# The last feed-forward's output product as seven block products of half size, with raw activations

## The chip, the cores and the metric

The kernel runs on one core of one Trainium2 chip. Its engines are named as in the profile: PE is the matrix engine (TensorE) and PEld its weight load, DVE the vector engine, ACT the scalar engine, POOL the GpSimd engine, SP the sync engine. SP and POOL issue the DMAs here. The metric is the time of one execution on the device in microseconds; three runs of the kernel before the change had a median of 1910.15 us (1910.07 to 1911.91).

## What is computed

A decoder trunk of two layers on 512 tokens of width 1024. Each layer is a half-step SwiGLU feed-forward, a mixing sub-layer (attention, RWKV-7, short convolution), and a second half-step feed-forward. Before each stands an RMS norm with a scale and shift from the conditioning vector c (adaLN); a gate from c scales what is added to the residual h.

```python
for l in range(DEPTH):                    # 2
    mod = (silu(c) @ w_ada[l] + b_ada[l]).reshape(B, 9, D_MODEL)
    ...
    hn = rms_norm(h, g_ffn2[l]) * (1.0 + sc3) + sh3
    h = h + 0.5 * (1.0 + gt3) * swiglu(hn, w_ffn2_in[l], w_ffn2_out[l])

def swiglu(x, w_in, w_out):               # 1024 -> 2 x 2816 -> 1024
    gate, up = split(x @ w_in, 2)
    return (silu(gate) * up) @ w_out
```

All data are float32.

## The kernel before

Everything is kept transposed: features on the 128 partitions, the 512 tokens along the free axis. h is eight tiles of 128 x 512; the 2816 inner features are 22 row tiles (NF), taken two at a time as 11 pairs.

A float32 product is made of three passes in the faster type fp32r. Weights and activations are each split into a high part (a cast on ACT, L104, or L455 and L557 for activations) and the rest (a subtraction on DVE, L105, or L456 and L558). The three matmuls are high x high, high weight x low activation, and low weight x high activation (`mm3`, L93 to L95; `mm6`, L101; `prod`, L449 to L451). So each weight tile costs a DMA into `wraw`, an ACT cast into `wH` and a DVE subtraction into `wL`; `wH` and `wL` have four buffers each, `wraw` has two.

A feed-forward (`ffn`, L370) works in two groups (GROUPS: row tiles 0 to 11, then 12 to 21). In each group it first makes the activations. The first two pairs (four in the very first feed-forward) go through plain products of 512 tokens (L538 to L559). Every later pair goes through `pair_in` (L458), which already forms its input product from seven block products instead of eight (a scheme of the Strassen kind): halves of the input features against halves of the tokens, 24 matmuls of 256 columns for each. For it, sums of weight blocks are made on the way in: a plain DMA on SP (`raw`), then a DMA on the POOL queue that adds a second block to it (`plus`, L403). The seventh product of a pair (`rest`, L515) is delayed into the next pair by `waiting` and `flush`. The pair's activations are split at once by `put` (L454) and kept as `actH` and `actL`.

Then the group multiplies its activations by the output weights (L578 to L591): for each of the eight output tiles, 12 or 10 row tiles times three matmuls of 512 columns into one PSUM bank, then a DVE update of h (`residual`, L315) with the gate `cg`. In the second group the last two output tiles go through `close` (L326) in token halves of 256 columns. Output tile by output tile, the first group also computes some rows of the adaLN vectors for later sub-layers (`ada_steps`, L176): POOL issues a load of 128 x 1024 weights `wada` into one of three buffers, and DVE makes a dot product of it (L168). `need` says how many rows must be done before a sub-layer ends.

The code names engines and tiles; a scheduler that runs when the program is built sets the order of each engine's queue, from dependences, buffers and its own estimates. Each engine then executes its queue strictly in order and waits on semaphores.

Of the kernel before, what the change touches and what calls it, by code (L numbers as in the profile page):

```python
# [16 lines left out]
P = 128  # L17
# [43 lines left out]
def trunk_kernel(ctx, tc, ins, out, layers=L, phases=("ffn1", "mix", "ffn2")):  # L61
# [308 lines left out]
    def ffn(l, w_in, w_pair, w_out, hn, im, ss, need, then, ready, first=None, late=None):  # L370
# [6 lines left out]
        with tc.tile_pool(name="act", bufs=1) as ap_:  # L377
            com = {n: tuple(ap_.tile([P, 4, H2], F32R, name=x, tag="com", bufs=8) for x in ("comH", "comL")) for n in ("P1", "P2", "T3", "T4")}
            ap_.tile([P, (512 - GAP) // 4], F32, name="gap", tag="gap")
            n_first = 2 if first is None else 4  # L380
            tiles = (t for t in projector([w_in[l, j, g] for j in range(2 * n_first) for g in range(2)], hn, BANKS[:3], first, 1, ready) if t is not None)
            xs, waiting, done, after = {}, [], [None], [None]
# [19 lines left out]
            def plus(w, src):  # L402
                nc.gpsimd.dma_start(w, src, accum_op=ALU.add)  # L403

            def new_x(p):

                X = tuple(ap_.tile([P, 2, T], F32R, name=x, tag="act", bufs=12) for x in ("actH", "actL"))
# [4 lines left out]
            rows_, sums = [], {}  # L412

            def whole(n):

                for k in (2 * n, 2 * n + 4):
                    x = ap_.tile([P, 2, T], F32, name="x", tag="act", bufs=12)
# [35 lines left out]

            def put(X, sl, x):  # L454
                nc.scalar.copy(X[0][:, :, sl], x)  # L455
                return tt(X[1][:, :, sl], x, X[0][:, :, sl].bitcast(F32), ALU.subtract)  # L456

            def pair_in(p):  # L458
# [52 lines left out]
                act(s2, s2, AF.Silu)  # L511
                tt(up, s2, up, ALU.mult)
                put(X, hi_, up)

                def rest():  # L515
                    prod(pD, hl(raw(A(1, 1))), T4, False)
                    tt(gate, pD, gate, ALU.mult)
                    return put(X, lo_, gate)

                waiting.append(rest)  # L520

            turn_ = [0]
# [12 lines left out]
            crep = ada_crep(ap_) if n_first == 4 else None  # L535
            for g, (j0, j1) in enumerate(GROUPS):
                for p in range(j0 // 2, j1 // 2):
                    if p < n_first:  # L538
                        X = new_x(p)
                        for j in (2 * p, 2 * p + 1):  # L540
# [13 lines left out]
                            else:  # L554
                                act(s, pg, AF.Silu)
                                stt(s, s, -1.0, pu, ALU.mult, ALU.mult)
                                nc.scalar.copy(xs[j][0], s)  # L557
# [4 lines left out]
                    else:  # L562
                        after[0] = None if g or p > n_first + 1 else loads[-2]
                        pair_in(p)
                        after[0] = None
                flush()
                if g and ss is not None:
# [768 lines left out]
    for n, (l, p) in enumerate(seq):  # L1336
# [25 lines left out]
    for i in range(KD):  # L1362
        nc.sync.dma_start(out[i], h[i])


def lay_out(i):
# [18 lines left out]
    for n, w in (("w1o", "w_ffn1_out"), ("w2o", "w_ffn2_out")):  # L1385
        a[n] = c(i[w].reshape(L, NF, P, KD, P).transpose(0, 3, 2, 1, 4))


# [62 lines left out]
```

## Time and profile before

| what | us |
|---|---|
| median of three runs | 1910.15 |
| the profiled execution: its span, first to last instruction | 1906.7 |
| the last feed-forward's pairs of the first group begin | 1607.4 |
| its first output group | 1685.35 to 1750.64 |
| its second group's pairs | 1750.64 to 1847.47 |
| its second output group, 512 columns | 1847.47 to 1888.28 |
| the same in `close`, 256 columns | 1888.28 to 1902.56 |

Times in the profile count from the span's start. A row of the table by stretch gives, for each engine, its busy time and instructions in that stretch, then the granted PE clock, the mean busy share of the 16 DMA engines, and what they moved in GB/s. A row of a group gives an instruction's line, engine, operation, tiles and shapes, its count, and behind the bar its busy time and the mean of one in ns, then the idle time before and what ended it.

### The profile page before, as it was taken

What the parts mean: (1) busy time and instruction counts of PE and PEld (TensorE: products, weight loads), DVE (VectorE), ACT (ScalarE), POOL (GpSimd) and SP (SyncE); (2) the same over time, 40 slices, a digit from 0 to 9 for tenths busy, and PEclk for the clock granted to TensorE, in tenths of its full rate; (3) what the DMA queues carried; (4) which work ended last, traced back from release to release, by engine and by line L of the source; (5) the groups of instructions that cost most, each with busy time, mean ns of one, the idle gap of its engine ahead of it and who ended that gap; (6) DMA issues with size and microseconds to landing.
All of it is one profiled execution on the core that took longest, in us unless ns stands there. A gap on an engine that the chain in (4) does not pass through costs nothing. (4 is left out here: it accounts for less than half of the span.)

```text
span 1906.7 us, 37156 instructions
## 1 busy us (share of the span) xinstructions
PE 1880.9 (99%) x15540; PEld 1742.4 (91%) x15540; DVE 1406.9 (74%) x2192; ACT 844.7 (44%) x1272; POOL 130.8 (7%) x212
## 2 busy tenths in 40 slices
PE   9999999999999999999999999999999999999999
PEld 8998899897889999899899989989877999988998
DVE  6797687858876877677777776877598777864862
ACT  4453355346432554155345524544553335532551
POOL 0101100000000000110100021010000000110000
PEclk8999999999999999999999999999999999999999
DMA  7667877421222476886717678781221306774741
GB/s 301 231 187 234 258 197 238 160 70 45 74 64 65 119 203 173 281 220 191 274 59 188 172 260 246 192 271 53 89 63 43 108 24 170 203 221 130 194 140 60
DMA packets 105864, 308.48 MB, mean 162 GB/s; under 512 B 23392, under 2 KB 26464, under 8 KB 104672
## 3 DMA queue, kind: packets, MB, share of 16 engines
q1 hardware_dynamic: 77472, 203.33, 32.6%
q0 software_dynamic: 28224, 102.77, 21.7%
q8 instruction: 122, 2.00, 0.4%
q14 instruction: 46, 0.38, 0.1%
HBM read 302.66 MB, written 3.41 MB: 161 GB/s over the span
## 5 line engine op out<-in xcount | busy, mean ns | idle before, releaser
L104 ACT CAST wH<-wraw 128x1024 fp32r<-128x1024 f32 (+2 forms) x292 | 268.5, 922 | 472.8 <-PE ps_mm L94 165.9
L105 DVE TENSOR_TENSOR wL<-wraw,wH 128x1024 fp32r<-128x1024 f32 (+2 forms) x292 | 308.3, 1059 | 99.5 <-ACT wH L104 98.6
L93 PE MATMUL ps_mm<-actH,wH 128*128 128x512 f32 (+1 forms) x784 | 288.6, 368 | 0.0
L94 PE MATMUL ps_mm<-actL,wH 128*128 128x512 f32 (+1 forms) x784 | 288.1, 368 | 0.0
L95 PE MATMUL ps_mm<-actH,wL 128*128 128x512 f32 (+1 forms) x784 | 288.1, 367 | 0.0
L449 PE MATMUL ps_d<-comH,wH 128*128 128x256 f32 x816 | 227.0, 278 | 1.9 <-ACT wH L104 0.8
L451 PE MATMUL ps_d<-comH,wL 128*128 128x256 f32 x816 | 225.9, 277 | 2.3 <-DVE wL L105 2.3
L450 PE MATMUL ps_d<-comL,wH 128*128 128x256 f32 x816 | 225.6, 277 | 0.0
L168 DVE SCALAR_TENSOR_TENSOR wada<-wada,crep 128x1024 f32<-128x1024 f32 x140 | 167.7, 1220 | 47.0 <-DMA wada<-in_wadaT 46.7
L101 PE MATMUL ps_mm<-hnH,wL 128*128 128x256 f32 x976 | 199.8, 283 | 0.5 <-DVE wL L105 0.5
L101 PE MATMUL ps_mm<-hnH,wH 128*128 128x256 f32 x976 | 197.7, 283 | 0.5 <-ACT wH L104 0.3
L101 PE MATMUL ps_mm<-hnL,wH 128*128 128x256 f32 x976 | 197.2, 281 | 0.0
L105 DVE TENSOR_TENSOR wL<-sum,wH 128x1024 fp32r<-128x1024 f32 x102 | 124.9, 1224 | 72.7 <-ACT wH L104 72.5
L95 PEld LDWEIGHTS ps_mm<-actH,wL 128*128 128x128 f32 x784 | 147.8, 189 | 24.5
L94 PEld LDWEIGHTS ps_mm<-actL,wH 128*128 128x128 f32 x784 | 147.8, 189 | 24.2
L93 PEld LDWEIGHTS ps_mm<-actH,wH 128*128 128x128 f32 x784 | 147.8, 189 | 24.0
L104 ACT CAST wH<-sum 128x1024 fp32r<-128x1024 f32 x102 | 107.5, 1054 | 136.0 <-PE ps_d L450 53.4
L449 PEld LDWEIGHTS ps_d<-comH,wH 128*128 128x128 f32 x816 | 153.3, 188 | 4.3 <-ACT s L487 1.8
L101 PEld LDWEIGHTS ps_mm<-hnH,wL 128*128 128x128 f32 x976 | 149.8, 188 | 7.9 <-issue 6.7
L101 PEld LDWEIGHTS ps_mm<-hnH,wH 128*128 128x128 f32 x976 | 148.9, 188 | 8.3 <-issue 5.1
L451 PEld LDWEIGHTS ps_d<-comH,wL 128*128 128x128 f32 x816 | 153.2, 188 | 2.9 <-DVE wL L105 2.9
L101 PEld LDWEIGHTS ps_mm<-hnL,wH 128*128 128x128 f32 x976 | 149.6, 188 | 5.2 <-issue 4.9
(433 smaller groups left out, 4338.4 us busy)
## 6 DMA issues: line engine op xcount, KB each, us to landing
wada<-in_wadaT POOLq DMA_DIRECT2D x128, 512.0 KB, 5.0
wraw<-in_wmi SPq DMA_DIRECT2D x40, 512.0 KB
wraw<-in_w2p SPq DMA_DIRECT2D x36, 512.0 KB
wraw<-in_w1p SPq DMA_DIRECT2D x32, 512.0 KB
wraw<-in_w1o SPq DMA_DIRECT2D x32, 384.0 KB
wraw<-in_w2o SPq DMA_DIRECT2D x32, 384.0 KB
wraw<-in_w1i SPq DMA_DIRECT2D x20, 512.0 KB
wraw<-in_w1o SPq DMA_DIRECT2D x32, 320.0 KB
```

The costliest lines, as they stand in the source:

```text
L93: mm(acc, wH, xH, start=start, stop=False)
L94: mm(acc, wH, xL, start=False, stop=False)
L95: mm(acc, wL, xH, start=False, stop=stop)
L101: mm(acc[:, sl], w[a][:, k], x[b][:, sl], start=start and n == 0 and sl is HALVES[0], stop=stop and n == 2, skip_group_check=True)
L104: nc.scalar.copy(hi, src)
L105: return nc.vector.tensor_sub(lo, src, hi.bitcast(F32))
L168: stt(w, w, 1.0, crep, ALU.mult, ALU.mult, accum_out=out_)
L449: mm(pt[:, i], wH, x[k][0], start=start and i + k == 0, stop=False, skip_group_check=True)
L450: mm(pt[:, i], wH, x[k][1], start=False, stop=False, skip_group_check=True)
L451: last = mm(pt[:, i], wL, x[k][0], start=False, stop=k == 3, skip_group_check=True)
```

## The change

In the last feed-forward alone (`whole_k`, where no statistics `ss` for a next norm are wanted) there is one group of all 22 row tiles, and the output product runs once, at the end, as seven block products. The blocks are: the halves of the output features (four tiles each), even and odd row tiles of the inner features, and the halves of the tokens. Each block product is 4 output tiles x 11 row tiles x 3 matmuls of 256 columns.

- Activations are no longer split when they are made. `put` and the first two pairs write them in float32 into `raw` tiles (four row tiles each); `corner` replaces the even tiles' second token half by odd minus even. In `halves` they are split later, for each product anew: a and b are the even and odd tiles' first token half, d the corner, c the odd tiles' second half; three products take combinations (a+d-c, -(a+d), a+d-b).
- Weights come from a copy `w2s` laid out by blocks. `weights` loads single blocks through `wraw`; the sums S, then S0, then S1 stay in one tile for each unit and are changed by adding DMAs on POOL; S3 is loaded in pieces of 128 x 512 into tiles `sumk` that take the place of the normed input (`hn`).
- A product runs in six units (five of two pairs of row tiles, one of one). `prepare` makes weights and activations two units ahead in program order. `finish` adds a product to h with the gate's columns, and stores a half row once nothing more comes to it. The last product runs its last two units output tile by output tile.
- The eight rows of the last gate, which were computed in the last feed-forward's first group, move ahead: four instead of three adaLN rows for each of the first four output tiles of the first group, in the second feed-forward of layer 0 and the first of layer 1 (and `need` of the latter is raised).

```diff
+            whole_k = ss is None
...
+            def corner(X):
+                return tt(X[:, 0, hi_], X[:, 1, hi_], X[:, 0, hi_], ALU.subtract)
...
+            def put(X, sl, x, y):
+                if whole_k:
+                    done_ = tt(X[:, :, sl], x, y, ALU.mult)
+                    return corner(X) if sl is hi_ else done_
...
+            def out_strassen(rest, raws):
...
+                pD, pF, pG = ([psum([P, 2, H2], n, t) for _ in range(2)] for n, t in (("ps_d", "x"), ("ps_f", "mm"), ("ps_g", "r0")))
...
+                def weights(name, u):
+                    n = 4 * size[u]
+                    pair = tuple(wp.tile([P, KD, P], F32R, name=x, tag=x, bufs=4) for x in ("wH", "wL"))
+                    at = lambda a, b: [x[:, a:b] for x in pair]
+                    if name == "S3":
+                        for k in range(size[u]):
+                            w = hnp.tile([P, 4, P], F32, name="sumk", tag="hn")
+                            kk = slice(2 * u + k, 2 * u + k + 1)
+                            nc.sync.dma_start(w, ws[0, 0, :, kk].rearrange("p k m c -> p (k m) c"))
+                            plus(w, ws[1, 0, :, kk].rearrange("p k m c -> p (k m) c"))
+                            split(*at(4 * k, 4 * k + 4), w)
+                        return pair
+                    if type(name) is tuple:
+                        w = wp.tile([P, KD, P], F32, name="wraw", tag="wraw", bufs=2)
+                        nc.sync.dma_start(w[:, :n], block(u, *name))
+                    elif name == "S":
+                        if u < 5:
+                            w = ap_.tile([P, KD, P], F32, name="sum", tag=("crep", "sum1", "first", "third", "sum0")[u], bufs=1)
+                        else:
+                            w = hnp.tile([P, 4, P], F32, name="sumk", tag="hn")
+                        S_[u] = w
+                        nc.sync.dma_start(w[:, :n], block(u, 1, 0))
+                        plus(w[:, :n], block(u, 1, 1))
+                    else:
+                        w = S_[u]
+                        plus(w[:, :n], block(u, *{"S0": (0, 0), "S1": (0, 1)}[name]))
+                    split(*at(0, n), w[:, :n])
+                    return pair
+
+                def halves(name, u):
...
+                    x = ap_.tile([P, 2, 2, H2], F32R, name="xs", tag="com", bufs=8)
...
+                    if src is None:
+                        src = E("xsum").rearrange("p (i t) -> p i t", i=2)[:, :n]
+                        if name == "a-c":
+                            tt(a, a, d, ALU.add)
+                        tt(src, a, c if name == "a-c" else b, ALU.subtract)
+                    split(xH, xL, src)
+                    return x
+
+                plan = (((0, 0), "a", pD, True, 0, lo_, False), ("S", "a-c", pF, True, 1, hi_, False), ("S0", "-a", pD, False, 0, hi_, False),
+                        ((0, 1), "b", pG, True, 0, lo_, True), ("S3", "d", pD, False, 1, hi_, True), ("S1", "c", pF, False, 0, hi_, True),
+                        ((1, 1), "a-b", pD, False, 1, lo_, True))
...
+                def run(q, us, ms):
+                    pt, start = plan[q][2:4]
+                    for m in ms:
+                        for u in us:
+                            (wH, wL), x = ready_[q, u]
+                            for k in range(size[u]):
+                                for n, (w, y) in enumerate(((wH, 0), (wH, 1), (wL, 0))):
+                                    mm(pt[m // 2][:, m % 2], w[:, 4 * k + m], x[:, y, k], start=start and u + k + n + m % 2 == 0, stop=u == NU - 1 and n == 2, skip_group_check=True)
+
+                def finish(q, ms):
+                    _, _, pt, _, half, sl, ends = plan[q]
+                    for m in ms:
+                        i = 4 * half + m
+                        stt(h[i][:, sl], pt[m // 2][:, m % 2], cg[:, i : i + 1], h[i][:, sl], ALU.mult, ALU.add)
+                        if ends:
+                            nc.sync.dma_start(out[i, :, sl], h[i][:, sl])
+
+                rest(lambda: [prepare() for _ in range(2)])
+                over = None
+                for q in range(len(plan)):
+                    end = q == len(plan) - 1
+                    for u in range(NU - 2 * end):
+                        prepare()
+                        if over is not None and u == 1:
+                            finish(over, range(4))
+                        run(q, (u,), range(4))
+                    over = q
+                for m in range(4):
+                    run(over, (NU - 2, NU - 1), (m,))
+                    finish(over, (m,))
...
-            for g, (j0, j1) in enumerate(GROUPS):
+            for g, (j0, j1) in enumerate(((0, NF),) if whole_k else GROUPS):
...
-                        many = 3 if not g else (2, 3, 3, 3, 3, 2)[i] if n_first == 4 else (3, 3, 3, 2, 2, 2)[i]
+                        many = (3, 4)[n_first == 2 and i < 4] if not g else (2, 3, 3, 3, 3, 2)[i] if n_first == 4 else (3, 3, 3, 2, 2, 2)[i]
...
-            w, need = ("w1", (l, 7)) if p == "ffn1" else ("w2", (l + 1, 1))
+            w, need = ("w1", (l, 7 + (l == layers - 1))) if p == "ffn1" else ("w2", (l + 1, 1))
```

Line numbers below are those of the changed kernel where a row is of it: there `plus` is L404, the sum of two products' inputs L596 and L597, the matmuls of the seven products L618, the update of h in them L624.

Three places in the order of the built program. First DVE, in the second feed-forward of layer 0, where the first output group begins; before:

```order
L168 SCALAR_TENSOR_TENSOR wada,mod_8_8777<-wada,crep 128x1024 x3
L105 TENSOR_TENSOR wL<-wraw,wH 128x768
L192 TENSOR_TENSOR mod_8_8777<-mod_8_8777,par 128x3
L586 TENSOR_SCALAR cg<-mod_8_8777 128x3
L315 SCALAR_TENSOR_TENSOR h_86<-ps_mm,cg,h_86 128x512
```

and of the change:

```order
L168 SCALAR_TENSOR_TENSOR wada,mod_8_8779<-wada,crep 128x1024 x3
L105 TENSOR_TENSOR wL<-wraw,wH 128x768
L168 SCALAR_TENSOR_TENSOR wada,mod_8_8779<-wada,crep 128x1024
L192 TENSOR_TENSOR mod_8_8779<-mod_8_8779,par 128x4
L105 TENSOR_TENSOR wL<-wraw,wH 128x768
L714 TENSOR_SCALAR cg<-mod_8_8779 128x4
L315 SCALAR_TENSOR_TENSOR h_86<-ps_mm,cg,h_86 128x512
```

A fourth dot product stands behind the first weight split, and the second split and the update of h stand behind it.

Second SP, at the seam from the last pair to the output product; before, where `wraw<-in_w2o` are the output weights:

```order
L399 DMA third<-in_w2p 128x1024
L399 DMA wraw<-in_w2p 128x1024
L272 DMA wraw<-in_w2o 128x640 x12
L1363 DMA out<-h_86 128x512
L272 DMA wraw<-in_w2o 128x640 x2
```

and of the change, where L575 loads S, L562 a piece of S3, and L568 a single block:

```order
L400 DMA third<-in_w2p 128x1024
L575 DMA sum<-in_w2s 128x1024 x2
L400 DMA wraw<-in_w2p 128x1024
L575 DMA sumk<-in_w2s 128x512
L568 DMA wraw<-in_w2s 128x1024
L562 DMA sumk<-in_w2s 128x512 x2
L575 DMA sum<-in_w2s 128x1024
L562 DMA sumk<-in_w2s 128x512
L575 DMA sum<-in_w2s 128x1024
L562 DMA sumk<-in_w2s 128x512 x2
L568 DMA wraw<-in_w2s 128x1024 x2
L562 DMA sumk<-in_w2s 128x512 x2
```

The loads of S and of the fifth product's S3 now stand between the last pair's last weights, the first product's first unit, and its second and third.

Third PE, at the end of the last product, with the waits; xs_21791 is its fifth unit, xs_21826 its sixth, and the PSUM tile ps_d_20461 holds output tiles 0 and 1, ps_d_20462 tiles 2 and 3. Before, the last 30 matmuls of `close` wait for nothing. Of the change:

```order
L618 MATMUL ps_d_20462<-xs_21791,wL_21786 128x256
L618 MATMUL ps_d_20461<-xs_21791,wH_21785 128x256 [waits DVE_49]
L618 MATMUL ps_d_20461<-xs_21791,wH_21785 128x256
...
L618 MATMUL ps_d_20461<-xs_21826,wL_21821 128x256
L618 MATMUL ps_d_20462<-xs_21826,wH_21820 128x256 x2
L618 MATMUL ps_d_20462<-xs_21826,wL_21821 128x256
L618 MATMUL ps_d_20462<-xs_21791,wH_21785 128x256 [waits DVE_49]
L618 MATMUL ps_d_20462<-xs_21791,wH_21785 128x256
```

Tile 1 now starts only when DVE has updated h from tile 0, which shares its PSUM tile, and tile 3 when it has updated h from tile 2; six matmuls of tile 2 were put ahead of tile 1.

More of the change, by code (lines that the diff above doesn't have):

```diff
@@ L412, in ffn @@
             rows_, sums = [], {}
+            free_rows = [new_raw()[:, i] for _ in range(2) for i in range(2)] if whole_k else []
+            raws_.clear()
             def whole(n):
                 for k in (2 * n, 2 * n + 4):
-                    x = ap_.tile([P, 2, T], F32, name="x", tag="act", bufs=12)
+                    x = free_rows.pop(0) if whole_k else ap_.tile([P, 2, T], F32, name="x", tag="act", bufs=12)
                     for i in range(2):
@@ L511, in pair_in, with rest, block, prepare @@
                 act(s2, s2, AF.Silu)
-                tt(up, s2, up, ALU.mult)
-                put(X, hi_, up)
-                def rest():
+                put(X, hi_, up, s2)
+                def rest(between=None):
                     prod(pD, hl(raw(A(1, 1))), T4, False)
-                    tt(gate, pD, gate, ALU.mult)
-                    return put(X, lo_, gate)
+                    if between:
+                        between()
+                    return put(X, lo_, gate, pD)
                 waiting.append(rest)
+            def out_strassen(rest, raws):
+                cg = small_.tile([P, KD], F32, name="cg", tag="cg")
+                for c, v in ((slice(0, 4), -0.5), (slice(4, 8), 0.5)):
+                    ts(cg[:, c], mod[l, im + 2][:, c], v, v, ALU.mult, ALU.add)
+                pD, pF, pG = ([psum([P, 2, H2], n, t) for _ in range(2)] for n, t in (("ps_d", "x"), ("ps_f", "mm"), ("ps_g", "r0")))
+                ws, NU = ins["w2s"], len(raws)
+                tall = [slice(2 * u, min(2 * u + 2, NF // 2)) for u in range(NU)]
+                size = [s.stop - s.start for s in tall]
+                S_, ready_ = {}, {}
+                def block(u, *names):
+                    return ws[names[0], names[1], :, tall[u]].rearrange("p k m c -> p (k m) c")
+                def weights(name, u):
[27 more added lines that the diff above has]
+                def halves(name, u):
+                    n, R = size[u], raws[u]
+                    a, d, b, c = (R[:, :n, i, sl] for i in range(2) for sl in (lo_, hi_))
+                    x = ap_.tile([P, 2, 2, H2], F32R, name="xs", tag="com", bufs=8)
+                    xH, xL = (x[:, i, :n] for i in range(2))
+                    if name == "-a":
+                        nc.scalar.mul(xH, a, -1.0)
+                        stt(xL, a, -1.0, xH.bitcast(F32), ALU.mult, ALU.subtract)
+                        return x
+                    src = {"a": a, "b": b, "c": c, "d": d}.get(name)
+                    if src is None:
[4 more added lines that the diff above has]
+                    split(xH, xL, src)
+                    return x
+                plan = (((0, 0), "a", pD, True, 0, lo_, False), ("S", "a-c", pF, True, 1, hi_, False), ("S0", "-a", pD, False, 0, hi_, False),
+                        ((0, 1), "b", pG, True, 0, lo_, True), ("S3", "d", pD, False, 1, hi_, True), ("S1", "c", pF, False, 0, hi_, True),
+                        ((1, 1), "a-b", pD, False, 1, lo_, True))
+                units = [(q, u) for q in range(len(plan)) for u in range(NU)]
+                def prepare():
+                    if units:
+                        q, u = units.pop(0)
+                        ready_[q, u] = weights(plan[q][0], u), halves(plan[q][1], u)
+                def run(q, us, ms):
[26 more added lines that the diff above has]
+                    finish(over, (m,))
@@ L555, in ffn @@
                                 act(s, pg, AF.Silu)
+                                if whole_k:
+                                    behind = stt(X[:, j % 2], s, -1.0, pu, ALU.mult, ALU.mult)
+                                    if j % 2:
+                                        corner(X)
+                                    beside(2 * j + 1)
+                                    continue
                                 stt(s, s, -1.0, pu, ALU.mult, ALU.mult)
@@ L565, in ffn @@
                         after[0] = None
+                if whole_k:
+                    return out_strassen(waiting.pop(), raws_)
                 flush()
@@ L1361, in trunk_kernel @@
         hn, ready = (nxt[0], (ws, marks)) if nxt else (None, None)
-    for i in range(KD):
-        nc.sync.dma_start(out[i], h[i])
 def lay_out(i):
```

9 lines of the change are left out of this document (8 added, 1 removed).

## The prediction

> **What bounds the kernel now.** First the head of the page, then its slices.
>
> ```profile
> span 1906.7 us, 37156 instructions
> PE 1880.9 (99%) x15540; PEld 1742.4 (91%) x15540; DVE 1406.9 (74%) x2192; ACT 844.7 (44%) x1272; POOL 130.8 (7%) x212
> PEclk8999999999999999999999999999999999999999
> DMA  7667877421222476886717678781221306774741
> ```
>
> TensorE is busy all the time, at the full granted clock but for the first slice. A busy PE could still be a waiting one, so next comes the table by stretch over the last feed-forward: its first output group, the pairs behind it (restart and steady part), the second output group in wide and in narrow matmuls, and the end.
>
> ```profile
> core 0: us, PE busy (x) PEld busy (x) DVE busy (x) ACT busy (x) POOL busy (x), PEclk, DMA share, GB/s
> 1685.35:1750.64 65.29, 65.29 (x290) 54.07 (x289) 34.88 (x50) 14.93 (x18) 5.24 (x8) 1.00 0.64 187
> 1750.64:1771.14 20.50, 20.06 (x170) 19.66 (x169) 12.60 (x13) 9.86 (x12) 1.70 (x2) 1.00 0.70 171
> 1771.14:1847.47 76.33, 76.33 (x675) 76.33 (x673) 59.47 (x65) 44.78 (x59) 4.29 (x5) 1.00 0.61 166
> 1847.47:1888.28 40.81, 40.81 (x182) 33.79 (x181) 15.04 (x20) 8.80 (x13) 0.00 (x0) 1.00 0.29 89
> 1888.28:1902.56 14.28, 14.28 (x121) 14.27 (x119) 2.20 (x4) 0.00 (x0) 0.00 (x0) 1.00 0.10 38
> 1902.56:1906.70 4.14, 0.28 (x3) 0.07 (x1) 0.48 (x1) 0.00 (x0) 0.00 (x0) 0.79 0.17 63
> ```
>
> By the loops the first row holds 8 x 12 x 3 = 288 matmuls of 512 columns (its edges cut one more on each side), so one takes 65.29/288 = 226.7 ns; the fourth 6 x 10 x 3 = 180, again 226.7 ns. The third holds 28 block products of 24 matmuls of 256 columns: 76.33/672 = 113.6 ns. A column costs the same in both, 0.443 ns. Nothing waits in these rows. PE's waits from the first pair on are short:
>
> ```profile
> PE ps_d L451 <- DVE wL L105: 0.8, 1, 0.8
> PE ps_d L449 <- ACT s L487: 0.4, 1, 0.4
> PE ps_d L449 <- ACT wH L104: 0.3, 1, 0.3
> ```
>
> So the bound is the number of columns that TensorE streams, and only a change in that number, or a new wait, moves the end.
>
> **The change, part by part. (1) The output product.** It takes away 65.29 + 40.81 + 14.28 = 120.38 us. It puts in seven products of 4 output tiles x 11 pairs of row tiles x 3 = 132 matmuls of 256 columns, 924 in all. At the steady 113.6 ns they take 104.97 us. The gain is 15.4 us: 528 matmuls of 512 columns, or 1056 of 256, become 924, seven eighths. Other prices: the narrow matmuls at the end of before take 14.28/120 = 119 ns, which would make 109.96 us. I take 113.6 because those rows have the same form (token half, own weight load, three in a row), precede the new stage without a break, and number 672; the 119 ns followed a stage of wide matmuls.
>
> [...]
>
> **(2) The break between the groups** goes. Its restart (second row) took 20.50 us for seven products of 24; at 113.6 ns they are 19.08. That gives 1.4 us. The start of the first pair, which holds the three waits above, stays; those waits could shrink by up to 1.5 us, as DVE has less to do there, and I count nothing.
>
> **(3) Feeding the seven products.** A product is fed in six units (five of two pairs, 24 matmuls or 2.73 us; one of half that). DVE and ACT work by these rows:
>
> ```profile
> L105 DVE TENSOR_TENSOR wL<-sum,wH 128x1024 fp32r<-128x1024 f32 x10 | 12.3, 1225 | 4.7 <-ACT wH L104 4.7
> L104 ACT CAST wH<-sum 128x1024 fp32r<-128x1024 f32 x10 | 10.6, 1056 | 13.0 <-PE ps_d L450 8.0 <-PE ps_f L450 5.0
> L456 DVE TENSOR_TENSOR actL<-gate,actH 128x512 fp32r<-128x512 f32 x5 | 3.4, 684 | 0.0
> L455 ACT CAST actH<-gate 128x512 fp32r<-128x512 f32 x5 | 3.1, 617 | 0.7 <-DVE gate L517 0.7
> L315 DVE SCALAR_TENSOR_TENSOR h<-ps_mm,cg,h 128x256 f32<-128x256 f32 x4 | 1.9, 484 | 12.2 <-PE ps_mm L95 12.2
> ```
>
> Seven products are 38.5 full units. DVE: 38.5 x (1.225 + 0.684) for the low parts of weights and activations, 16.5 x 0.684 for a+d, a-c and a-b, 28 x 0.484 for h: 98 us, against 105 us of PE. ACT: 38.5 x 1.673 = 64 us. The tight product is the second: 5.5 x (1.225 + 3 x 0.684) + 4 x 0.484 = 20.0 us of DVE beside 15.0 of PE. The first needs 10.5 without h updates, so 4.5 us are left over there, and four buffers of wH and wL let DVE run three units, 8.2 us, ahead. The 5 us are covered; without that cover they would cost 5 us. PE's queue holds nothing else meanwhile.
>
> Transfers: each quarter of the weights is 2.88 MB. Plain loads are five quarters, additions on the POOL queue four. Their rates, first an addition with no other transfer, then the fastest mixture:
>
> ```profile
> 1784.80:1788.20 3.40, 3.40 (x33) 3.40 (x32) 2.41 (x3) 1.66 (x2) 0.00 (x0) 1.00 1.04 205
> 15.00:30.00 15.00, 15.00 (x97) 14.33 (x90) 9.83 (x19) 4.48 (x8) 0.00 (x0) 0.69 1.03 415
> ```
>
> So 14.4/0.415 + 11.5/0.205 = 34.7 + 56.1 = 91 us of full DMA, in 105 us and some 15 us of lead. Most of it stands early: the SP queue issues the fifth product's eleven S3 halves among the first product's loads, and POOL adds to them before it gets to S0. Six of the eleven wait for hn tiles that the last pair reads until about 3 us before its end. From the last pair's second product, 16 us before the seam, to 15 us behind it, SP carries 15.5 whole units of 512 KB (S 2.5, S3 5.5, first product 5.5, fourth 2) and POOL 8 (S 2.5, S3 5.5): 15.5 x 1.26 + 8 x 2.56 = 40 us of DMA in 31 us. What can be late is S3's additions, which nobody needs for 60 us, but by SP's order also the wraw loads of the first product's fourth to sixth unit. Behind the wait for such a load stand, on DVE, the splits of the next units. The overhang of 9 us against the lead of 8.2 us bounds the wait at some 3 us once the six late S3 halves are taken off the front; at the other end nothing waits. I take 0.7, nearer that end, since most of the overhang is additions that nobody waits for.
>
> **(4) The end.** The last update and store stay as they were:
>
> ```profile
> 1902.56 0.28 PE L95 MATMUL ps_mm<-actH,wL 128*128 128x256 f32 x1
> 1902.87 0.48 DVE L315 SCALAR_TENSOR_TENSOR h<-ps_mm,cg,h 128x256 f32<-128x256 f32 x1 [3.11 <-PE ps_mm L95]
> 1903.38 0.33 SPq L1363 DMA_DIRECT2D out<-h  x1
> ```
>
> New are two PE waits for a DVE update of the same PSUM tile. Output tile 1 starts behind six matmuls of tile 2, which hide it; tile 3 has no cover: from last matmul to the end of the update 0.79 us, less one matmul. Cost 0.8 us (0 to 1.5). Only the last nine matmuls and the store queue behind it.
>
> **(5) Four adaLN rows instead of three** for four output tiles, in the second feed-forward of layer 0 and the first of layer 1.
>
> ```profile
> 754.03 1.22 DVE L168 SCALAR_TENSOR_TENSOR wada<-wada,crep 128x1024 f32<-128x1024 f32 x1
> 768.35 1.22 DVE L168 SCALAR_TENSOR_TENSOR wada<-wada,crep 128x1024 f32<-128x1024 f32 x1
> 769.50 1.22 DVE L168 SCALAR_TENSOR_TENSOR wada<-wada,crep 128x1024 f32<-128x1024 f32 x1
> 769.87 0.53 POOL L182 DMA_DIRECT2D wada<-in_wadaT  x1 [4.04 <-DVE wada L168]
> 772.01 1.23 DVE L168 SCALAR_TENSOR_TENSOR wada<-wada,crep 128x1024 f32<-128x1024 f32 x1 [1.29 <-DMA wada<-in_wadaT]
> 773.23 0.95 DVE L105 TENSOR_TENSOR wL<-wraw,wH 128x768 fp32r<-128x768 f32 x1
> wada<-in_wadaT POOLq DMA_DIRECT2D x12, 512.0 KB, 5.1
> 759.30:783.80 24.50, 24.50 (x109) 20.27 (x108) 18.54 (x33) 5.06 (x7) 4.75 (x9) 1.00 0.89 291
> 800.10:808.30 8.20, 8.20 (x38) 6.77 (x37) 2.94 (x4) 1.78 (x2) 0.00 (x0) 1.00 1.00 345
> ```
>
> The eight rows that these add leave the last feed-forward's wide group, where they hid under PE; taking them there saves nothing. Here three buffers bound the rate: dot 1.2 + 0.3 until POOL issues (768.35 + 1.22 to 769.87) + landing 5.1 = 6.6 us a turn, so four dots take 8.8 us beside 8.16 us (65.29/8) of PE. Sixteen dots fall 2.6 us behind. Behind a waiting dot stand, on DVE, the weight splits of the tiles after next. Counting from the first dot, the split at risk (second half of the sixth tile, behind dot 19) is ready after 18 x 2.2 + 1.2 + 0.95 = 41.8 us; PE needs it 5.5 x 8.16 us after the group's start at 751.15, that is 42.0 us after the dot at 754.03. At 6.6 us a turn nothing waits; at 7.0, 2.2 us. The traffic would rise from 291 to about 330 GB/s, close to the 345 at which the DMA share is 1.00, so landings get longer. Both places: 0 to 6 us; I take 1.5.
>
> **Sum**, against the profiled execution: 1906.7 - 120.4 - 1.4 + 105.0 + 0.7 + 0.8 + 1.5 = 1892.9 us. The median of the runs is 1910.15, 3.45 us above the span; with the same distance, 1896.3 us.
>
> **Rivals.** *Narrow matmuls dearer* (119 ns, part 1): 5.0 us more, 1901.3 us. For it: that row, and no other work was on DVE or ACT there. Against: every steady pair. [...] *Feeding decides*: the dot ring at 7.3 us a turn or the seam's transfers 5 us late, each about 4 to 6 us: 1902 us. For it: DMA share 0.89 already with three dots, and the 40 us in 31. Against: leads of 8 us, and PE waits of nearly nothing today. *Additions one at a time, slower than before*: if an addition started only when the one before has landed, the POOL queue would set the time.
>
> ```profile
> 1780.90 0.85 POOL L403 DMA_DIRECT2D third<-in_w2p  x1 [17.29 <-DMA third<-in_w2p]
> 1783.10 0.86 POOL L403 DMA_DIRECT2D sum<-in_w2p  x1 [1.36 <-DVE sum L473]
> sum<-in_w2p POOLq DMA_DIRECT2D x2, 512.0 KB, 6.5
> ```
>
> There are 15 whole and 14 half additions; at 6.5 and, halved in bytes, some 5.2 us that is 170 us, while S1 must be in after about 104 us from the first: some 60 us late, about 1955 us. It decides from a mean of 3.6 us per addition. Against it: the second of these rows was issued 2.2 us after the first, before that could have landed, and the 205 GB/s above, 2.6 us per 512 KB. That it removes fewer matmuls than it says is excluded: the built program has 924 of the new line.
>
> **How the numbers follow.** Forecast 0.64; dearer matmuls 0.12; feeding 0.17; additions in series 0.03; a wait that I haven't seen 0.04, half of it large. The range runs from 1892.5 (no waits in parts 3 and 5, and the first pair's waits gone) to 1904 (the second and third case, with some of both). Within 0.2% of before, 3.8 us, is about what a measurement of this kernel can't tell from no change. Faster by more: 0.93; within it: 0.03; slower: 0.04.
>
> **What would show it.** Right: 924 matmuls of the new line over 105 to 107 us; PE's waits in it under 2 us; the wide groups of the two earlier feed-forwards still 65.3 us. Wrong: a stretch of that stage over 115 ns per matmul with PE waiting for nothing (dearer matmuls); waits of wL or wH on DMA in the first two products, or a wide group of 68 us (feeding); POOL issues spaced by their landings (series).

## The result and the profile after

The change made the kernel slower: 1926.38 us (median of 4 runs) against 1910.11 us, a ratio of 1.0105 (95% interval 1.0088 to 1.0122). The forecast was 1896.3 us, faster. Head and slices of the page after:

```profile
span 1925.9 us, 38035 instructions
PE 1876.3 (97%) x15876; PEld 1750.9 (91%) x15876; DVE 1448.6 (75%) x2260; ACT 868.7 (45%) x1306; POOL 155.6 (8%) x241
PEclk8999999999999999989999999999999999999999
```

TensorE now works 1876 us of 1926, and the clock drops in one more slice, in the middle. The table by stretch, columns as in the prediction, gives in this order: the wide group of layer 0's second feed-forward and the start of the pairs behind it, the wide group of layer 1's first, the last feed-forward's pairs, and the output product in three pieces (first product; second and third; the other four).

```profile
749.33:822.42 73.09, 68.47 (x290) 55.74 (x289) 53.62 (x89) 14.75 (x18) 14.27 (x25) 0.95 0.83 271
822.42:850.00 27.58, 24.32 (x185) 24.11 (x184) 15.50 (x16) 11.60 (x15) 1.72 (x2) 0.88 0.71 182
1106.88:1181.87 74.99, 68.09 (x290) 54.92 (x289) 53.66 (x87) 14.80 (x18) 14.18 (x25) 0.98 0.80 264
1628.87:1802.21 173.34, 172.32 (x1514) 171.92 (x1513) 128.94 (x139) 89.67 (x110) 21.28 (x25) 1.00 0.74 204
1802.21:1828.44 26.23, 19.81 (x134) 18.39 (x133) 13.62 (x20) 8.67 (x12) 6.12 (x8) 0.87 1.05 267
1828.44:1860.32 31.88, 30.59 (x267) 30.18 (x265) 29.88 (x44) 19.19 (x27) 10.26 (x12) 1.00 1.03 197
1860.32:1922.16 61.84, 60.97 (x530) 60.16 (x528) 42.50 (x66) 30.09 (x45) 0.00 (x0) 1.00 0.38 117
```

Set against the stages of before (a stage runs from its first matmul to that of the next):

| stage | before | after | difference | forecast |
|---|---|---|---|---|
| wide group, layer 0 second feed-forward | 65.30 | 73.09 | +7.8 | together +1.5 |
| all pairs behind it | 96.65 | 102.08 | +5.4 | |
| wide group, layer 1 first feed-forward | 65.29 | 74.99 | +9.7 | |
| last feed-forward's pairs (77.94 + 96.83 before) | 174.77 | 173.34 | -1.4 | -1.4 |
| output product | 120.38 | 119.95 | -0.4 | -13.9 |

Together these are 21.1 us; the rest of the program was 1.9 us shorter in this profile, so the span grew by 19.2. So two things went wrong: the adaLN rows cost 22.9 us, not 1.5, and the output product lost in waits nearly all that it gained in columns. PE's waits in it, with what ended them, their sum, how many there were and the longest:

```profile
PE ps_d L618 <- ACT wH L104: 3.9, 3, 2.6
PE ps_d L618 <- DVE wL L105: 2.5, 4, 0.8
PE ps_f L618 <- DVE wL L105: 1.3, 1, 1.3
PE ps_d L618 <- DVE h L624: 0.6, 1, 0.6
```

### The profile page after: what moved, and what is told of

It reads as the page before. It is cut to its first block, busy times and chain, and to the rows that moved or that the text cites. A ratio compares the mean times of both kernels' runs of the same rounds, so it can differ in the third digit from the quotient of the medians.

```text
span 1925.9 us, 38035 instructions
## 1 busy us (share of the span) xinstructions
PE 1876.3 (97%) x15876; PEld 1750.9 (91%) x15876; DVE 1448.6 (75%) x2260; ACT 868.7 (45%) x1306; POOL 155.6 (8%) x241
## 3 DMA queue, kind: packets, MB, share of 16 engines
HBM read 316.55 MB, written 3.41 MB: 166 GB/s over the span
## 4 chain that ended last, share of the span: by engine, by line
PE 43%; DVE 5%; DMA 3%; issue 3%; ACT 1%; POOL 0%; SPq 0%; ACTq 0%; POOLq 0%; DVEq 0%
PE ps_mm L101 6%; PE ps_d L463 4%; PE ps_d L465 4%; PE ps_d L464 4%; PE ps_mm L93 3%; PE ps_mm L95 3%; PE ps_mm L94 3%; PE ps_d L618 3%; PE ps_f L465 2%; PE ps_f L463 2%; PE ps_f L464 2%; PE ps_f L618 2%; DMA wraw<-in_w2s 1%; DVE wL L105 1%; DMA wada<-in_wadaT 1%
## 5 line engine op out<-in xcount | busy, mean ns | idle before, releaser
L104 ACT CAST wH<-wraw 128x1024 fp32r<-128x1024 f32 (+3 forms) x278 | 261.3, 941 | 462.6 <-PE ps_mm L94 114.8
L105 DVE TENSOR_TENSOR wL<-wraw,wH 128x1024 fp32r<-128x1024 f32 (+3 forms) x278 | 300.2, 1084 | 99.0 <-ACT wH L104 98.3
L95 PE MATMUL ps_mm<-actH,wL 128*128 128x512 f32 (+1 forms) x588 | 218.5, 372 | 11.5 <-DVE wL L105 11.5
L93 PE MATMUL ps_mm<-actH,wH 128*128 128x512 f32 (+1 forms) x588 | 218.2, 371 | 0.0
L94 PE MATMUL ps_mm<-actL,wH 128*128 128x512 f32 (+1 forms) x588 | 217.6, 370 | 0.0
L105 DVE TENSOR_TENSOR wL<-sum,wH 128x1024 fp32r<-128x1024 f32 x117 | 143.1, 1223 | 74.6 <-ACT wH L104 74.5
L104 ACT CAST wH<-sum 128x1024 fp32r<-128x1024 f32 x117 | 123.2, 1053 | 148.9 <-PE ps_d L464 62.3
L464 PEld LDWEIGHTS ps_d<-comL,wH 128*128 128x128 f32 x816 | 154.3, 189 | 0.0
L95 PEld LDWEIGHTS ps_mm<-actH,wL 128*128 128x128 f32 x588 | 111.8, 190 | 32.5 <-DVE wL L105 14.1
L94 PEld LDWEIGHTS ps_mm<-actL,wH 128*128 128x128 f32 x588 | 111.9, 190 | 18.7
```

The lines of the kernel that those rows point to most:

```text
L93: mm(acc, wH, xH, start=start, stop=False)
L94: mm(acc, wH, xL, start=False, stop=False)
L95: mm(acc, wL, xH, start=False, stop=stop)
L104: nc.scalar.copy(hi, src)
L105: return nc.vector.tensor_sub(lo, src, hi.bitcast(F32))
L464: mm(pt[:, i], wH, x[k][1], start=False, stop=False, skip_group_check=True)
```

## The experiments

In the tables below a wide group or a product is measured as above. First a set that takes the two causes apart.

**The rows alone (e1).** The kernel before with two lines changed:

```diff
-                        many = 3 if not g else ...
+                        many = (3, 4)[n_first == 2 and i < 4] if not g else ...
-            w, need = ("w1", (l, 7)) if p == "ffn1" else ...
+            w, need = ("w1", (l, 7 + (l == layers - 1))) if p == "ffn1" else ...
```

> The kernel before, with only the eight adaLN rows moved; the last feed-forward is the old one. If the moved rows cost what the changed kernel's trace shows in the two wide groups (73.1 and 75.0 us instead of 65.3, and 5.5 us in the pairs behind the first), the two groups are again 72 to 75 us long and the time is about 1910 + 22 = 1932 us, 1.1% slower than before. Rival: the long groups come from something else in the changed program; then both groups stay at 65.3 us and the time at 1910 us.

1926.43 us, ratio 1.0104 (1.0080 to 1.0127). The rows alone make the kernel as slow as the whole change did, though not as slow as the 1932 us expected. Table by stretch of e1: first wide group, all pairs behind it, second wide group, and the last feed-forward's group that gave its rows away.

```profile
748.21:819.03 70.82, 67.50 (x290) 55.03 (x289) 53.29 (x88) 14.81 (x18) 13.39 (x24) 0.98 0.84 278
819.03:918.29 99.26, 95.99 (x842) 95.59 (x840) 72.69 (x78) 53.30 (x69) 8.57 (x11) 1.00 0.73 202
1101.02:1177.03 76.01, 69.15 (x290) 55.37 (x289) 54.28 (x88) 14.81 (x18) 14.29 (x25) 0.96 0.81 263
1701.46:1766.76 65.30, 65.30 (x291) 54.06 (x290) 26.44 (x30) 15.53 (x19) 0.86 (x1) 1.00 0.41 114
```

Against 65.3, 96.65 and 65.3 that is 5.5 + 2.6 + 10.7 = 18.8 us. The last row stays at 65.3: there the rows had been free.

**The rows in the pairs (e2).** The changed kernel with three rows per tile again; the eight rows go to the pairs of the last feed-forward (of the edit, the part in the loop over pairs):

```diff
...
+                        if whole_k and p < 7:
+                            spare_ = [raws_[n][:, 1].rearrange("p i t -> p (i t)") for n in (4, 5)]
+                            with tc.issue_after(done[0].ins) if done[0] else nullcontext():
+                                if p > n_first:
+                                    ada_rows(spare_, crep)
+                                else:
+                                    crep = ada_crep(ap_)
+                                if todo:
+                                    ada_loads(spare_)
...
```

> The changed kernel with the row move undone: three rows per output tile as before, and the eight rows of the last gate computed in the last feed-forward's pairs three to six, two per pair, in halves of tiles that are empty until pair eight. If the moved rows cost 22 us, both wide groups are back at 65.3 us and the time is 1926 - 22 + 0 to 3 = 1904 to 1908 us; the output product still takes 120 us. Rival: rows cost the same wherever they stand (DVE has not the time); then the pairs get some 10 to 20 us longer and the time stays at 1920 us or more.

1906.11 us (10 runs), ratio to before 0.9992 (0.9983 to 1.0002). Wide groups, pairs and output product of e2:

```profile
746.86:812.15 65.29, 65.29 (x290) 54.07 (x289) 45.79 (x79) 13.53 (x17) 12.22 (x21) 1.00 0.84 270
1091.56:1156.85 65.29, 65.29 (x290) 54.05 (x289) 46.04 (x78) 13.84 (x17) 12.15 (x21) 1.00 0.83 268
1605.75:1779.09 173.34, 172.32 (x1515) 171.92 (x1513) 137.36 (x165) 89.54 (x110) 26.77 (x34) 1.00 0.84 232
1779.09:1900.88 121.79, 111.10 (x925) 108.19 (x924) 85.99 (x128) 57.83 (x84) 16.28 (x19) 0.97 0.70 168
```

Both groups are whole again, and the pairs take 173.34 us with the rows as without: DVE has the time (137.4 us busy), and the loads have room (a DMA share of 0.84). The rows' work can be had for nothing; what cost the time was the place they were put in.

**Why four rows did not fit (e6, e7, e9).** All three are e1 with one thing more: in e6 the first `sum` addition of the pairs stands behind the last rows' loads on POOL; in e7 the load of the fourth row is left out wherever four are taken at once (so also twice in the first feed-forward), and the third row's buffer is used once more; in e9, on top of e7, the first pair's `third` stands ahead of the second pair's `sum` on SP and POOL, where the scheduler had turned them round. The column beside the pairs says whether the buffer of `third` is given back first, second or last of the three at that seam; it is explained below.

```diff
# e6, in plus
+                with tc.issue_after(last_row[0].ins) if last_row[0] else nullcontext():
                     nc.gpsimd.dma_start(w, src, accum_op=ALU.add)
```

```diff
# e7, in ada_steps
+            if len(cols) == 3:
+                cols.append(cols[-1])
+                continue
```

```diff
# e9, in pair_in; third_ holds the two DMAs of the pair before
+                if p == 7 and n_first == 2:
+                    after[0] = third_[0]
                 S = raw(A(1, 0), ("sum0", "sum1")[p % 2])
...
+                with tc.issue_after(third_[1].ins) if p == 7 and n_first == 2 else nullcontext():
                     plus(S, A(1, 1))
```

> The kernel before with the moved rows (e1), but the first addition of the next group's pair stands behind the last adaLN loads of the wide group on POOL instead of ahead of three of them. If the waits at the last tile (2.5 and 4.1 us, with the half clock behind the longer one) come from this addition, which waits 7 to 8 us for its plain load with the rows' loads behind it, they go and the two groups are 67 to 70 us long instead of 70.8 and 76.0; the pairs behind may lose a little. Rival: the ring of three buffers alone; then the groups stay as they are.

> The kernel before with the moved rows (e1), but the fourth row of a tile is not loaded: its dot product is made of the third row's buffer once more, so DVE does the same and the loads are those of three rows. If the turn of the buffers and the DMA cost the time, both groups are back at 65.3 us and the time at some 1908 us. Rival: DVE's own time for four dots; then the groups stay above 70 us.

> e7 (the moved rows in the kernel before, the fourth of a tile not loaded), with the order at the seam behind the wide group put back: on SP and POOL the first pair's third sum ahead of the second pair's first, as before the change. In e7 the wide groups were 67.1 and 67.2 us, but the pairs behind them 104.9 and 102.8 us instead of 96.6 and 96.2. If the scheduler's other order costs this, the pairs return to 96 to 97.5 us, the wide groups stay at 67, and the time is some 1909 to 1911 us. Rival: the pairs wait because everything is late behind the rows; then they stay above 101 us.

| | first wide group | pairs behind | `third` | second wide group | pairs behind | `third` | time, us |
|---|---|---|---|---|---|---|---|
| before | 65.30 | 96.65 | first | 65.29 | 96.23 | first | 1910 |
| changed | 73.09 | 102.08 | last | 74.99 | 96.29 | second | 1926.4 |
| e1 | 70.82 | 99.26 | last | 76.01 | 96.38 | second | 1926.4 |
| e6 | 68.30 | 102.26 | last | 69.30 | 96.27 | second | 1915.7 |
| e7 | 67.12 | 104.93 | last | 67.22 | 102.77 | last | 1923.7 |
| e9 | 66.15 | 103.18 | last | 69.91 | 100.46 | last | 1921.3 |

e6, e7 and e9 are one run each, so their times have no interval and the stages are what is read. e6 came out as expected: one addition ahead of three loads was worth 9 us of wide groups, of which 3 us came back as longer pairs. e7 came out only in part: the groups lost most of their excess, which speaks for the loads and the turn of the buffers, since DVE's own time, the rival, would have left the groups above 70 us; but the pairs took 12 us more than in e1, and the time stayed. My next guess, the scheduler's other order, fell in e9: the pairs still wait. The rival written there, that everything is late behind the rows, cannot be all either: e1's second wide group ended 10.7 us late, and the pairs behind it took 96.4 us. The traces of the changed kernel and of the one before show more. First POOL's queue in the changed kernel, the first load of each turn of four and the end of the group; then in the kernel before, the first load of two turns of three, and the end.

```profile
759.11 0.53 POOL L182 DMA_DIRECT2D wada<-in_wadaT  x1 [2.56 <-DVE mod L192]
768.36 0.53 POOL L182 DMA_DIRECT2D wada<-in_wadaT  x1 [1.68 <-DVE wada L168]
777.47 0.53 POOL L182 DMA_DIRECT2D wada<-in_wadaT  x1 [2.50 <-DVE mod L192]
786.68 0.53 POOL L182 DMA_DIRECT2D wada<-in_wadaT  x1 [2.35 <-DVE mod L192]
...
793.92 0.53 POOL L182 DMA_DIRECT2D wada<-in_wadaT  x1 [1.69 <-DVE wada L168]
801.85 0.88 POOL L404 DMA_DIRECT2D sum<-in_w2p  x1 [7.40 <-DMA sum<-in_w2p]
803.42 1.60 POOL L182 DMA_DIRECT2D wada<-in_wadaT  x3 [0.68 <-DVE mod L192]
```

```profile
778.03 0.53 POOL L182 DMA_DIRECT2D wada<-in_wadaT  x1 [3.96 <-DVE wada L168]
...
786.19 0.53 POOL L182 DMA_DIRECT2D wada<-in_wadaT  x1 [3.62 <-DVE wada L168]
...
797.30 1.93 POOL L182 DMA_DIRECT2D wada<-in_wadaT  x3
```

Three rows a turn go with PE's 8.16 us (778.03 to 786.19); four take 9.1 to 9.25. The only turn of three ahead of the seam, 786.68 to 793.92, won back 0.9. The last three loads leave 54.1 us after the group's start instead of 46.1, 8 us later: the plain load of `sum` is late with the rows, and POOL stands 7.4 us ahead of its addition instead of 5.6. Behind those loads stand DVE's last dots, and behind these the last weight split and SP's loads for the next pairs. DVE, then PE with the ACT cast that it waits for in the pairs, then SP in the changed kernel, and last SP in the kernel before:

```profile
811.33 1.23 DVE L168 SCALAR_TENSOR_TENSOR wada<-wada,crep 128x1024 f32<-128x1024 f32 x1 [6.54 <-DMA wada<-in_wadaT]
812.62 1.23 DVE L168 SCALAR_TENSOR_TENSOR wada<-wada,crep 128x1024 f32<-128x1024 f32 x1
813.86 1.23 DVE L168 SCALAR_TENSOR_TENSOR wada<-wada,crep 128x1024 f32<-128x1024 f32 x1
815.08 0.95 DVE L105 TENSOR_TENSOR wL<-wraw,wH 128x768 fp32r<-128x768 f32 x1
```

```profile
816.09 0.79 PE L95 MATMUL ps_mm<-actH,wL 128*128 128x512 f32 x1 [4.37 <-DVE wL L105]
...
829.81 1.04 ACT L104 CAST wH<-third 128x1024 fp32r<-128x1024 f32 x1 [6.32 <-DMA third<-in_w2p]
...
832.83 0.58 PE L463 MATMUL ps_d<-comH,wH 128*128 128x256 f32 x1 [3.27 <-ACT s L490]
```

```profile
812.60 0.33 SPq L400 DMA_DIRECT2D sum<-in_w2p  x1
813.88 0.33 SPq L400 DMA_DIRECT2D first<-in_w2p  x1
815.12 0.33 SPq L400 DMA_DIRECT2D third<-in_w2p  x1
```

```profile
807.16 0.33 SPq L399 DMA_DIRECT2D third<-in_w2p  x1
808.61 0.33 SPq L399 DMA_DIRECT2D sum<-in_w2p  x1
809.87 0.33 SPq L399 DMA_DIRECT2D first<-in_w2p  x1
```

The rows and the pairs take the same three buffers (tags `first`, `third`, `sum1`), so each of these loads starts the moment a dot ends (in the changed kernel the dots end at 812.56, 813.85 and 815.09). That carries the lag into the pairs, where ACT's cast of `third` comes late and PE, behind the copy that ACT makes after it, waits 3.27 us.

Which buffer comes back first depends on how many rows were loaded up to the seam, since the rows take the three in turn: 69 in the kernel before, 73 in the changed one. So `third` came back first before and last after, and its addition landed 3.3 and 7.3 us behind the first matmul of the pairs. e7 and e9 change this place too: with 67 rows loaded up to the first seam (two fewer in the first feed-forward) and 103 up to the second, `third` came back last in both, and e9's new order could not bring its load forward. Over the seams of all eleven kernels the pairs took 99.3 to 104.9 us in the nine cases with `third` last, and 96.2 to 97.1 us with `third` first or second in twelve of thirteen; the exception is in e8 (below). That goes with the place of `third`, not with the lag: the second wide groups of e1 and of the changed kernel were 10.7 and 9.7 us too long, and the pairs behind them took 96.4 and 96.3 us. No run changes this place alone, so it is not shown as the cause; a move of three or six rows would test it.

**The output product (e3, e4, e5, e8).** In e3 the loads of S3 stand on SP behind the first product's last load; e4 leaves out S3's additions; e5 is e2 with e3's edit, and S3's additions behind S0's on POOL; e8 is e5 with a third buffer for the fourth product.

```diff
...
# e3 and e5, in weights, for S3
+                            with tc.issue_after(singles[NU - 1].ins):
                                 nc.sync.dma_start(w, ws[0, 0, :, kk].rearrange("p k m c -> p (k m) c"))
# e5 alone
+                            with tc.issue_after(added[-1].ins):
                                 plus(w, ws[1, 0, :, kk].rearrange("p k m c -> p (k m) c"))
# e8, for single blocks
+                        if name == (0, 1) and u == 2:
+                            w = raws[5][:, 1].rearrange("p i (k c) -> p (i k) c", c=P)
...
```

> The changed kernel with the loads of S3 put on SP behind the last weight load of the first product instead of among them; the adaLN rows stay where the change put them. If S3's traffic at the seam delays the first products, their waits of 8.5 us and the half clock behind them (3 us) go, the output product falls from 120 to 107 to 110 us, and the time from 1926 to about 1914. Rival: DVE and ACT cannot feed the first two products faster; then it stays at 118 to 120 us. Second rival: S3 comes late instead and the fifth product waits; then the first two products are clean and the waits stand at the fifth.

> The changed kernel without the additions to S3: its second weight block is left out, so that the fifth product multiplies by one block alone; the plain loads stay where they are in SP's queue. If the eleven additions (2.9 MB, at 205 GB/s some 14 us of all DMA engines) are what crowds the seam, the output product falls from 120 to 106 to 110 us. Rival: it is the order of the plain loads on SP; then it stays near 118 us.

> The kernel with the rows in the pairs (e2), and the S3 work of the output product in the order in which it is needed: its plain loads behind the first product's last load on SP, and its additions behind those of S0 on POOL. In e3, where only the plain loads were moved, the first two products waited 2.1 us instead of 9.5, and the third and fourth 11.8, because S0's additions stood behind S3's on POOL. If it is this order that costs the time, the output product falls from 122 to 108 to 111 us and the time from 1906 to 1893 to 1896 us, which is 0.7 to 0.9% faster than before. Rival: the DMA engines have not the time at all; then the waits move to the fifth and sixth product, and it stays above 116 us.

> e5 with a third buffer for the fourth product's weights: its third unit is loaded early into the half tile that held adaLN rows, so that the loads of its fourth and fifth unit are issued one unit sooner, ahead of S1's additions. In e5 those loads, issued among the additions, took some 7 us and PE waited 3.2 and 1.0 us in the fourth product, with the half clock behind it 5.9 us more than steady. If that is the cause, the fourth product takes 15 to 16 us instead of 20.8, the output product 107.5 to 109 instead of 113.4, and the time falls from 1897 to 1891 to 1893 us. Rival: the DMA share of 1.0 delays whatever comes there; then the wait moves to the unit behind and the time stays at 1895 us or more.

| us | product 1 | 2 | 3 | 4 | 5 | 6 | 7 | together | time (ratio to before) |
|---|---|---|---|---|---|---|---|---|---|
| changed | 26.2 | 16.9 | 15.0 | 16.0 | 15.0 | 15.0 | 15.9 | 119.95 | 1926.4 (1.0105) |
| e2 | 26.8 | 16.9 | 15.0 | 17.2 | 15.0 | 15.0 | 16.0 | 121.79 | 1906.1 (0.9992) |
| e3 | 16.2 | 17.0 | 22.5 | 22.7 | 15.0 | 15.0 | 16.0 | 124.2 | 1931.3 (1.0125; 1.0104 to 1.0146) |
| e4 | 18.8 | 17.0 | 15.0 | 16.0 | 15.0 | 15.0 | 16.0 | 112.5 | 1914.1 (one run) |
| e5 | 15.3 | 16.5 | 15.0 | 20.8 | 15.0 | 15.0 | 16.0 | 113.4 | 1897.2 (0.9945; 0.9930 to 0.9959) |
| e8 | 15.1 | 16.5 | 15.0 | 15.3 | 15.6 | 15.6 | 16.4 | 109.4 | 1891.6 (0.9917; 0.9900 to 0.9934) |

Where PE waits for nothing, a product of the changed kernel takes 14.96 us (132 matmuls at 113.3 ns). There the table by stretch shows the 17 us ahead of the seam, the DMA issues of 1797 to 1805 their median landing times (last column), ACT's waits in the first two products what they wait for, and a row of ACT the longest of them:

```profile
1785.00:1802.21 17.21, 17.21 (x154) 17.21 (x153) 12.92 (x17) 8.31 (x12) 6.79 (x8) 1.00 0.98 284
```

```profile
sum<-in_w2s POOLq DMA_DIRECT2D x2, 512.0 KB, 11.3
sumk<-in_w2s POOLq DMA_DIRECT2D x3, 256.0 KB, 13.4
```

```profile
ACT wH L104 <- DMA wraw<-in_w2s: 15.5, 4, 9.1
...
1806.62 1.04 ACT L104 CAST wH<-wraw 128x1024 fp32r<-128x1024 f32 x1 [9.14 <-DMA wraw<-in_w2s]
```

The DMA engines are full from 17 us before the first product (a share of 0.98), and its weights come late: the load of its second unit, issued at 1793.76, is cast at 1806.62. Of the first product's 11.3 us over 14.96, e3 leaves 1.2 and e4 3.8, with DVE's and ACT's work unchanged. So most of it is S3's traffic, not the time of DVE or ACT. e4's whole product stays above the 106 to 110 us expected. And e3 as a whole is slower than the changed kernel: S3 does come late, as its second rival says, but the waits stand at the third and fourth product, not at the fifth. In the table by stretch, its first two products, then its third and fourth, and a piece of its POOL queue:

```profile
1803.01:1836.19 33.18, 31.53 (x266) 30.82 (x265) 30.51 (x45) 18.62 (x26) 10.37 (x12) 1.00 0.92 236
1836.19:1881.36 45.17, 35.34 (x266) 33.62 (x265) 25.24 (x38) 19.87 (x31) 9.44 (x11) 0.92 0.95 213
```

```profile
1815.79 0.86 POOL L404 DMA_DIRECT2D sumk<-in_w2s  x1 [15.07 <-DMA sumk<-in_w2s]
...
1821.02 0.86 POOL L404 DMA_DIRECT2D sum<-in_w2s  x1 [0.74 <-DVE wL L105]
1827.29 0.85 POOL L404 DMA_DIRECT2D sumk<-in_w2s  x1 [5.41 <-DMA sumk<-in_w2s]
```

POOL stood 15 us before an S3 addition whose plain load was now late, with S0's additions (`sum`), which the third product needs, queued behind it. e5 puts both queues in the order of need. The product falls to 113.4 us, not quite the 108 to 111 expected, and one long wait is left, in the fourth product:

```profile
1824.63:1845.46 20.83, 17.12 (x134) 16.72 (x133) 11.34 (x19) 9.95 (x17) 3.86 (x5) 0.92 1.07 253
```

There the DMA share is 1.07. POOL issues five of S1's additions from 1823.3 to 1829.5, as early as their tiles allow; the plain loads that SP issues behind them, at 1829.41 and 1832.14, land 8.0 and 8.5 us later. In e8 these loads leave one unit sooner; the share is as high and the wait is gone:

```profile
1833.44:1848.74 15.30, 15.24 (x135) 15.04 (x133) 8.56 (x14) 6.09 (x11) 3.52 (x5) 1.00 1.08 263
```

e8 is the fastest kernel here, 0.8% faster than the one before. In its profiled run (span 1900.0, above its median) the pairs behind layer 1's wide group took 101.3 us instead of 96.2, with three rows a tile as before and `third` given back first; its six runs spread from 1888 to 1902 us. So that seam can lose 5 us without a fourth row; why it does in some executions stays open. Its last three products took 15.6, 15.6 and 16.4 us, 118 ns a matmul, at the full granted clock and with no wait but the one at the end: 1.7 us more than at 113.3 ns. This dearer pace is near the 119 ns of the prediction's first rival, and what sets it stays open.

## Why the prediction was wrong

- **(1) The output product's columns**: right. Three of the seven products (the third, fifth and sixth) took 14.96 us, which is 113.3 ns a matmul, against 113.6 used, and the others are longer by their waits. The rival of dearer matmuls is out for the changed kernel. Why e8's last three products show its pace and these do not is open, so a part of this hit may be luck.
- **(2) The break between the groups**: right, 1.43 us against 1.4, and the first pair's waits stayed, as forecast.
- **(3) Feeding**: 0.7 us forecast (0 to 3), 14.2 measured (119.95 - 104.7, less the 1.0 us by which the seventh product is longer). The step that failed is "most of the overhang is additions that nobody waits for". The sum of 40 us of DMA in 31 was right: the share was 0.98 to 1.05 from 17 us before the seam on. But the full DMA engines did not serve by need here. Everything in flight was slow together: additions issued between 1797 and 1805 took 9.5 to 13.9 us to land (three of the five are half the size), where two of the kernel before took 6.5, and the plain load that PE needed was cast 12.9 us after its issue. So the overhang fell on the first product's weights as well, and that product's 11.3 us of excess are waits (7.9 us) and, for the rest, almost all the slow clock behind them. The other part, that DVE's 5 us of overload in the second product were covered, was 1.5 us short: that product takes 16.5 us and waits for wL even in e8.
- **(4) The end**: right, 0.8 us (a start-to-start of 0.91 us less one matmul).
- **(5) The adaLN rows**: 1.5 us forecast (0 to 6), 22.9 measured. Three things failed in it. A turn of four took 9.2 us, not 8.8, since a dot also waits in DVE's queue (the load issued at 779.47 landed 4.8 us later, and its dot began at 785.17, 0.9 us on, behind two splits), so that four tiles lost 4.2 us, not 2.6; the landings, which I had expected to get longer, took 4.8 us (median) from 759 to 793 us, against 5.1 before. The place was wrong, and this is the step that cost most: I asked only for the split of the sixth tile, where the margin was 0.2 us, and let the lag end there. At that split PE waited nothing in the first group and 1.9 us in the second; the long waits, 4.5 and 4.3 us, stood at the split of the eighth. For the lag is hardly won back, and meets at the seam a POOL addition that stands 7.4 us ahead of the last loads, and then loads that need the rows' buffers, `third` last. And half a clock, which the sum has at nothing, followed the long waits.
- **The rivals**: "feeding decides" named both places where the time was lost, at 1902 us and 0.17, and for the output product the right mechanism. For the rows it had a slower ring of buffers (7.3 us a turn, against some 6.9 here), not the seam. Its price was some 5 us where 37 were lost. Additions in series are out: POOL issued five within 8 us, each of which took 9.5 us or more to land.

## What to carry to other kernels

The lag of a stage whose turn was longer than PE's (9.2 us against 8.16) did not end at the first instruction that was late. Follow such a lag to the stage's end, and ask which queue entries and which buffers the next stage shares with it, and in which order these buffers come back when the count in a ring changes. Where the DMA engines are full (here a share of 0.98 to 1.05, with additions 9.5 to 13.9 us from issue to landing instead of 6.5), count every transfer in flight as late, and put each queue, SP's and POOL's, in the order of need: the same loads and additions, with one buffer more, took the output product from 122 us to 109. Work that is free in one place (eight rows under a wide group, or in the pairs) may cost 20 us in another, so price the place it goes to by running that move alone.

## What the runs showed of the hardware

The clock's answer to a wait. Table by stretch: the changed kernel behind a wait of 3.54 us and behind one of 2.14 us, then e6 behind one of 2.36 us.

```profile
832.83:838.60 5.77, 5.77 (x27) 5.77 (x28) 0.71 (x1) 0.41 (x1) 0.86 (x1) 0.50 0.72 201
1155.13:1158.50 3.37, 3.37 (x15) 2.79 (x16) 3.37 (x6) 0.00 (x0) 0.00 (x0) 1.00 0.79 275
```

```profile
1146.37:1149.82 3.45, 3.45 (x9) 2.67 (x10) 3.45 (x6) 0.00 (x0) 0.47 (x1) 0.53 0.80 258
```

In the changed kernel four waits (start-to-start gaps of 2.9 and, 0.2 us later, 1.0; 3.5; 4.5; 4.8 us) were each followed by 3.5 to 6 us at half clock. By the granted clock of these stretches that is 2.8 and 1.7 us in the wide groups, 2.9 in the pairs and 2.8 in the first product, 10 of the 38 us that waiting cost. Its record of the clock has, from 600 us of the span to the last matmul, these four half-clock stretches alone: three of 6.83 us and, in the second wide group, one of 3.41. The kernel before has none there, and no gap above 1.7 us. A wait of 2.14 us had no such price, one of 2.36 us in e6 had, and one of 3.47 us in e1 had none (3.2 us in the list of waits; the pairs that it stands in have a mean clock of 1.00). Longer ones, of 3.7 us in e1's second wide group, 6.0 in e7's first pairs and 3.9 in e3's fourth product, stand in stretches with a mean clock of 0.96, 0.97 and 0.92. So the length of the wait alone did not decide, and what did stays open. The forecast's sum has nothing for it.
